# A fourth pair of output tiles by seven quarter products, and a new order of the products in two pairs

## The chip, the core and the metric

The kernel runs on one core of one Trainium2 chip. The metric is the device time of one execution in microseconds: 726.66 us in the median of three runs before the change (726.62 to 727.09). The engines are PE (TensorE, matrix products, with its weight loads shown apart as PEld), DVE (VectorE), ACT (ScalarE), POOL (GpSimd) and SP (SyncE, which here only issues DMAs). They run side by side and wait for each other through semaphores. Each engine takes its own instructions strictly in order.

## The reference: what is computed

One layer of a decoder trunk, for one sequence of 1024 tokens and 1024 channels, in float32:

```
h  = rmsnorm(x) * (1 + scale(c)) + shift(c)
cv, cg, cs, lx, ls = split(h @ w_in)              # 5 x 1024 columns
v  = layernorm(causal_depthwise_conv31(cv * sigmoid(cg)))
y_conv = (silu(v) @ pw2 + b) * silu(cs)
xs = causal_depthwise_conv4(lx)
r, i = sigmoid(blockdiag(xs, wr)), sigmoid(blockdiag(xs, wi))
hs = linear_scan(a(r), sqrt(1 - a^2) * i * xs)
y_lru = hs * silu(ls)
x = x + (1 + gate(c)) * (concat(y_conv, y_lru) @ w_out)
out = rmsnorm(x)
```

The change concerns the product of `y_lru` (1024 channels, the "lru" half) with its half of `w_out`: 1024 x 1024 by 1024 x 1024.

## The kernel before, in words

**Layout.** Activations lie with channels on the 128 partitions and the 1024 tokens along the free axis: eight tiles of 128 x 1024. A matmul multiplies a 128 x 128 block of weights with 128 x 512 of an activation and adds into PSUM. Float32 accuracy is had by splitting each operand into a high part (rounded to fp32r) and a low part (the remainder): a product is three matmuls, high by high ("H"), high weight by low operand ("X") and low weight by high operand ("W"). Names follow this: `whi` and `wlo` for weights, `yh` and `yl` for the eight lru activations ("heads").

**Order of work.** All operations are first recorded with a priority and their reads and writes. A planner (`Plan.order`) then replays them with an estimated cost for each, and on every engine takes the ready operation of lowest priority number; this gives each engine one fixed order. A slot is one output tile of a plain product, 48 matmuls; slot n has priority n. Buffers are planned too. There are 47 large buffers of 128 x 1024 (`NBIG`) for activations, pools of two for raw, high and low weights (`raw`, `whi`, `wlo`), and in PSUM three full tiles (`mm`) and two half tiles (`acc`). Some operations must leave a reserve of large buffers free (`SPARE`).

**Stages on PE.** Slots 0 to 39 are the input projection with the small gate products between them. From slot 40 (`B0`) comes the lru half of `w_out`, eight tiles of 128 output channels: two slots for each pair of tiles. From priority 48 (`C0`) comes the pointwise product `pw2`, and from 56 (`D0`) the convolution half of `w_out`. Both of these use seven half-size products for each pair of tiles (tiles `xpw`, `ypw`, `zpw` and `xout`, `yout`, `zout`). Meanwhile DVE, ACT and POOL compute the depthwise convolution (tiles `c`), then its layer norm (tiles `mean`, `lnbc`, `lnss`), then the operands of `pw2` (`quarters`, tiles named `va`, `vb`, `vc`, `vT` with `h` or `l` for high or low). TLATE is by how much the operands that need differences stand behind the others in priority there and in the same function for the last stage.

**Pairs of lru tiles.** `lru_pair` (L1383 on) treats two output tiles together (`LRU_P = 3` pairs, then the last two tiles as plain slots 46 and 47). Of the eight contraction tiles, heads 0 to 3 (`JS = (0, 1)`, two couples) go by a Strassen-Winograd scheme: with the two output tiles, the two contraction tiles of a couple and the two halves of the tokens, each a 2 x 2 block matrix, seven quarter products stand for eight. Heads 4 to 7 go plainly. `LORDER` names the steps of a pair. Step p multiplies heads 4 to 7 for the first tile (24 matmuls, PSUM tile `lp`). q and r do so for the second tile's two token halves (12 each). 1, z, 2, 3, y, s and 4 are the quarter products of six matmuls each:

```
1: A11 B11 -> lx      z: A12 B21 -> lp       s: S4 B22 -> lp
2: S2 T2  -> lx       y: S1 T1  -> ly       3: S3 T3  -> lx     4: A22 T4 -> lx
```

A and S are weights (S are sums and differences of blocks), B whole operands and T differences of operands. After most steps the accumulator is copied out (`use`): the first copy into a block of the result `acc` is made by ACT with a scale, later ones are added by DVE. Later steps go on accumulating into the same PSUM tile, so they wait until it has been read: q follows y in `ly`, 3 follows 2 and 4 follows 3 in `lx`.

**Operands.** `lru_sums` makes the differences T for each couple (tiles `yhs`, `yls`). The S weights are prepared once, early, in `lru_prepare` (tiles `lz`, `lh`, `ll`, from slot `PREN = 5`), stored to DRAM (`lsdh`, `lsdl`) and loaded again as `lsh`, `lsl` before their pair. Other weights of a tile come as `raw`; ACT copies them to `whi`, writes the negated high part into `wlo`, and a DMA from POOL's queue adds the raw weights to that (`remainder`). With `LWB = "big"` high and low weights of all lru tiles take large buffers. `SPILL` lists finished convolution tiles that are stored to DRAM (`cd`) and loaded back (`cr`) to free their large buffer in between. `acc_store` adds a finished tile `acc` to a copy of x in DRAM.

Of the kernel before, what the change touches and what calls it, by code (L numbers as in the profile page):

```python
# [14 lines left out]
P = 128  # L15
D = 1024
T = 1024
KT = D // P
H = 512
# [21 lines left out]
SPARE = 5  # L41
# [5 lines left out]
UK = 7  # L47
HRES = 2
POOLED = (1, 3, 5)
TLATE = 2.5  # L50
QGATES = ((1, 5), (3, 0), (3, 2), (3, 4))
OUT_P = (0, 1, 2, 3)
HELD = (1, 2, 3)
# [23 lines left out]
NP = {0: (6, 0, 1), 512: (6, 0, 7), 768: (6, 0)}  # L77
SUMS = (2, 0, 4, 3, 1, 6, 7, 5)
CSD = 2
SPILL = (0,2,4)  # L80
SPP0, SPP1, SPN = 30, 40.5, 39
EVN = 4
CQR = 2
YHEADS, YSLOT = 2, 36
JS = (0, 1)
LRU_P = 3
NJ = len(JS)
LK = tuple(2 * j + z for z in (0, 1) for j in JS) + tuple(k for k in range(KT) if k // 2 not in JS)
LACT = ((0, 0), (0, 1), (1, 0), (1, 1))
LORDER = "p1zy2q3s4r"  # L90
LTP = 0.5
LTD = (2,1)
PREN, PRES = 5, 3
PREP, XCP = 18, 19
# [1 line left out]
XCN = 33  # L96
LEV = ()
LWB = "big"
LWO = 0.5
FINP = -0.5  # L100
BCLATE = False
BEHIND = 0
PLACED = ("big",)
MARGINS = 2.0
TERMS = {**{("pw2_0", c): ("HW", "X") for c in "1z"}, **{(f"out_{p}", "1"): ("HX", "W") for p in (0, 1, 2, 3)}, **{(f"pw2_{p}", "1"): ("HX", "W") for p in (1, 2, 3)}}
LTERMS = {}
LLATE = 45
SLOTT = {46: ("HX", "W"), 47: ("HX", "W")}
FINQ = 0.0
LRV = ()  # L110
# [250 lines left out]
def hymba_layer(ctx: ExitStack, tc: tile.TileContext, xT, vecs, mod_w, w_first, w_in,  # L361
# [25 lines left out]
    S = Plan(pools)  # L387
# [117 lines left out]
    B0, C0, D0 = 40, 48, 56  # L505
# [610 lines left out]
    v, c = {}, {}  # L1116
# [160 lines left out]
    def gates(i, n):  # L1277
        xs, xh, xl = lru[i]
        hi, lo = gw.pop(i)
        r, g, a = big_buf(f"r{i}"), big_buf(f"g{i}"), big_buf(f"a{i}")  # L1280
        for j, (dst, b) in enumerate(((r, "br"), (g, "bi"))):
            ps = mm_tile(f"gate{i}_{j}")

            def emit(j=j, ps=ps):
                for lhs, rhs, st in ((hi, xh, 0), (hi, xl, 1), (lo, xh, 2)):
                    for c0, c1 in FULL:
                        pe.matmul(ps()[:, c0:c1], lhs()[:, j, :], rhs()[:, c0:c1],  # L1287
                                  start=st == 0, stop=st == 2)
# [13 lines left out]
        t = sls.pop(i)  # L1302
        TT(pr, "DVE", t, t, r, ALU.mult, r=[t, r], w=[t])
        yh[i], yl[i] = big_buf(f"yh{i}", F32R, 2), big_buf(f"yl{i}", F32R, 2)
        o = split(B0 - 2 + 0.2 * i, yh[i], yl[i], t, reserve=SPARE)
        if i < YHEADS:
            waiting.append(o)
        if LRU_P and i // 2 in JS:
            ys[i] = t
            if i % 2:  # L1310
                lru_sums(i // 2)

    def lru_sums(j):
        pr, x0, x1 = B0 - 2 + 0.4 * j + LTP, ys[2 * j], ys[2 * j + 1]

        def sub(to, a, b):
            TT(pr, "DVE", half(*to), half(*a), half(*b), ALU.subtract, H, r=[a, b], w=[to])
        sub((x0, 0), (x0, 1), (x0, 0))
        sub((x0, 1), (x1, 1), (x0, 1))
        sub((x1, 1), (x1, 1), (x0, 0))  # L1320
        sub((x1, 0), (x1, 0), (x1, 1))
        sets = []
        for z, x in enumerate((x0, x1)):
            hi, lo = (big_buf(f"y{h}s{j}{z}", F32R, 2) for h in "hl")
            if j in LTD:
# [57 lines left out]
    def lru_pair(p, n, use, firsts):  # L1383
# [1 line left out]
        s0, s1 = ("lru", 2 * p), ("lru", 2 * p + 1)  # L1385
        q = n - 1.4 - LWO
        for s in (s0, s1):
            w_bufs(s, LWB)
            DMA(n - 2.5 - LWO, k3(raw[s]), lambda s=s: wsrc(s)[:, :, :], FULL_BYTES, w=[raw[s]])
        r0, r1 = raw[s0], raw[s1]  # L1390
        for s, k in ((s0, 0), (s1, NJ)):
            hi, lo, r = whi[s], wlo[s], raw[s]
            cut = lambda b, k=k: (lambda: k3(b)()[:, k:, :])
            keys = lambda b, k=k: [(b, i) for i in range(k, KT)]
            ACT(q, cut(hi), cut(r), "copy", (KT - k) * P, r=keys(r), w=keys(hi))
# [16 lines left out]
        def quarter(c, a, b, ps, h, begin):  # L1412
            wh, wl, i, key = wq[a]
            rk = [(wh, key), (wl, key)] if key is not None else kk(wh, i) + kk(wl, i)
            for j, (bh, bl) in enumerate(lsets[b]):
                def emit(j=j, bh=bh, bl=bl):
                    o = (i * NJ + j) * P
                    for lhs, rhs, t in ((wh, bh, 0), (wh, bl, 1), (wl, bh, 2)):
                        pe.matmul(half(ps, h)(), lhs()[:, o:o + P], half(*rhs)(),  # L1419
                                  start=begin and j == 0 and t == 0, stop=j == NJ - 1 and t == 2,  # L1420
                                  skip_group_check=True)
                o = S.op("PE", 3 * (H + 32) / 2400, emit, n + g, [*rk, bh, bl],
                         [(ps, h if ps.parts > 1 else 0)], columns=3 * H)
                ops.setdefault(c, o)

        for c in LORDER:
            g += 0.12
            if c == "p":
                groups = LTERMS.get(p, ("HXW",))
                for gr in groups:  # L1430
                    for k in rest:
                        o = mm_k(n + g, p0, s0, yh, yl, k, FULL, first=rest[0], group=gr,
                                 end=gr == groups[-1])
                        ops.setdefault(c, o)
            elif c == "q":
# [84 lines left out]
    for s in slots[4:]:  # L1520
# [5 lines left out]
        if s[0] == "pair":  # L1526
# [3 lines left out]
            def use(n, i, h, ps, key, s=s, ts=ts, begun=begun):  # L1530
                m, to, tk = 2 * s[1] + i, half(ts[i], h), (ts[i], h)
                if (i, h) not in begun:
# [5 lines left out]
                    return  # L1538
                STT(n + 0.5, to, ps, gate1[:, m:m + 1], to, ALU.mult, ALU.add, H,
                    r=[tk, key, ("gate1", m)], w=[tk])  # L1540
            started[n], started[n + 1] = lru_pair(s[1], n, use, [started[n - 2]])
            for m, t in zip((2 * s[1], 2 * s[1] + 1), ts):
                acc_store(n, m, t)
            n += 1
            continue
        if s not in NEXT:
            if s[0] == "lru":
                weights(s, n=n - LWO, eng="DVE" if s[1] in LRV else "DMA", where=LWB,
                        later=[started[LLATE]] if LLATE else [])
            else:  # L1550
                weights(s, late=[pending_evac[n]] if n in pending_evac else ())
# [243 lines left out]
```

## Time and profile before

| what | value |
|---|---|
| median of three runs | 726.66 us |
| the profiled execution | 726.9 us |
| its span, first to last instruction | 725.1 us |
| granted clock of TensorE, mean | 0.995 |
| PE, matmuls | 717.0 us busy, 99% |
| DVE | 617.8 us, 85% |
| ACT | 480.8 us, 66% |
| POOL | 170.8 us, 24% |
| HBM read, written | 79.37 MB, 21.50 MB |

The profile shows one execution. Busy time is what an engine spent in instructions; DMA-issuing ones are not counted. A row of the chain of waits has a start, a duration, and what the time went to; a row of the timeline adds the line in the kernel, the operation, `output<-inputs`, shapes, and how many instructions were merged. Matmuls overlap, so their pitch (start to start) is shorter than the duration of each. The share of busy time is a mean over stages, so each stage is looked at by itself.

### The profile page before, as it was taken

How to read it: one execution, taken by the hardware profiler on the slowest of the kernel's cores; microseconds unless marked ns; L12 is line 12 of the kernel's file. 1: busy time of each engine (PE TensorE's matmuls, PEld its weight loads, DVE VectorE, ACT ScalarE, POOL GpSimd, SP SyncE). 2: the span in 40 equal slices, each digit the busy share in tenths (PEclk: the TensorE clock that was granted, in tenths of full speed). 3: DMA queues.
4: the chain of work that ended last, by engine and by line, in shares of the span. 5: the costliest groups of instructions: out<-in, count | busy, mean ns of one | idle time of the engine just before them, and what ended most of it. 6: DMA issues, size and time to landing. Idle time of an engine off the chain costs nothing.

```text
span 725.1 us, 9076 instructions
## 1 busy us (share of the span) xinstructions
PE 717.0 (99%) x3274; PEld 597.5 (82%) x3274; DVE 617.8 (85%) x848; ACT 480.8 (66%) x615; POOL 170.8 (24%) x172
## 2 busy tenths in 40 slices
PE   9999999999999999999999999999999999999996
PEld 8888888888888888888888888888888888888885
DVE  7999999899799997688499995999789566999656
ACT  7650679655698857966949879858785345755322
POOL 0036233443543320233220220211021101100003
PEclk9999999999999999999999999999999999999997
DMA  9946348768899997799999597998867855774006
GB/s 341 408 169 169 43 112 234 191 120 200 180 246 209 264 220 194 172 221 217 193 217 301 111 188 172 253 239 230 190 103 160 228 120 143 223 190 176 23 17 215
DMA packets 46059, 137.80 MB, mean 190 GB/s; under 512 B 5200, under 2 KB 15824, under 8 KB 45904
## 3 DMA queue, kind: packets, MB, share of 16 engines
q0 software_dynamic: 20016, 54.84, 42.0%
q1 hardware_dynamic: 24992, 81.48, 32.3%
q10 hardware_dynamic: 1008, 0.92, 0.4%
q8 instruction: 25, 0.41, 0.2%
q14 instruction: 18, 0.15, 0.1%
HBM read 79.37 MB, written 21.50 MB: 139 GB/s over the span
## 4 chain that ended last, share of the span: by engine, by line
PE 96%; DVE 1%; ACT 1%; DMA 1%; issue 0%; POOL 0%; POOLq 0%
PE ps L560 57%; PE xout L736 6%; PE xpw L736 6%; PE first L867 5%; PE ypw L736 3%; PE gate L1287 3%; PE lp L560 2%; PE lx L1419 2%; PE zout L736 2%; PE zpw L736 2%; PE ly L560 1%; PE lx L560 1%; PE lp L1419 1%; PE yout L736 1%; PE late L867 1%; PE ly L1419 1%
## 5 line engine op out<-in xcount | busy, mean ns | idle before, releaser
L560 PE MATMUL ps<-uh,whi 128*128 128x512 f32 x576 | 177.4, 389 | 0.0
L560 PE MATMUL ps<-ul,whi 128*128 128x512 f32 x576 | 177.4, 389 | 0.0
L560 PE MATMUL ps<-uh,wlo 128*128 128x512 f32 x576 | 177.3, 389 | 0.0
L560 PEld LDWEIGHTS ps<-uh,wlo 128*128 128x128 f32 x576 | 108.1, 188 | 22.5
L560 PEld LDWEIGHTS ps<-ul,whi 128*128 128x128 f32 x576 | 108.1, 188 | 22.4
L560 PEld LDWEIGHTS ps<-uh,whi 128*128 128x128 f32 x576 | 108.0, 188 | 22.3
L405 ACT CAST whi<-raw 128x1024 fp32r<-128x1024 f32 (+1 forms) x44 | 45.1, 1031 | 48.7 <-PE ps L560 30.0
L437 POOL DMA_DIRECT2D es<-cq x45 | 41.0, 910 | 128.7 <-ACT cq L413 90.2
L432 POOL TENSOR_TENSOR wlo<-raw,whi 128x1024 fp32r<-128x1024 f32 x16 | 41.6, 2607 | 88.6 <-ACT whi L405 88.3
L413 ACT ACT_TABLE_LOAD x45 | 57.7, 1283 | 2.0 <-PEq L1787 0.7
L424 DVE SCALAR_TENSOR_TENSOR cacc<-v,V,cacc 128x511 f32<-128x511 f32 (+14 forms) x75 | 55.8, 744 | 0.5
L424 DVE SCALAR_TENSOR_TENSOR caccs<-v,V,caccs 128x511 f32<-128x511 f32 (+6 forms) x70 | 52.1, 745 | 2.2 <-ACT caccs L413 1.1
L424 DVE SCALAR_TENSOR_TENSOR caccs<-c,wsum,caccs 128x511 f32<-128x511 f32 (+6 forms) x70 | 52.1, 745 | 0.8
L437 POOL DMA_DIRECT2D oo<-co x39 | 37.0, 980 | 41.3 <-issue 10.6
L413 ACT ACTIVATE cq<-v,V 128x511 f32<-128x511 f32 (+14 forms) x45 | 31.8, 709 | 0.0
L424 DVE SCALAR_TENSOR_TENSOR xs<-ps,V,xs 128x1023 f32<-128x1023 f32 (+2 forms) x24 | 30.7, 1278 | 0.0
L424 DVE SCALAR_TENSOR_TENSOR modw<-modw,sc 128x1024 f32<-128x1024 f32 x23 | 29.6, 1289 | 0.2 <-DMA modw<-in_mod_w_dram 0.2
L413 ACT ACTIVATE cq<-c,wsum 128x512 f32<-128x512 f32 x42 | 29.7, 713 | 0.0
L432 DVE TENSOR_TENSOR wlo<-raw,whi 128x1024 fp32r<-128x1024 f32 x20 | 24.4, 1220 | 5.4 <-ACT whi L405 5.2
L413 ACT ACTIVATE co<-v,V 128x510 f32<-128x510 f32 (+12 forms) x39 | 27.0, 707 | 0.0
L413 ACT ACTIVATE finsq<-fin 128x512 f32<-128x512 f32 (+2 forms) x14 | 7.9, 570 | 27.4 <-DVE fin L424 14.3
L432 POOL TENSOR_TENSOR o<-fin,bc 128x256 f32<-128x256 f32 (+1 forms) x8 | 7.8, 994 | 68.6 <-ACT bc L405 63.0
(413 smaller groups left out, 1585.5 us busy)
## 6 DMA issues: line engine op xcount, KB each, us to landing
raw<-in_w_in_dram SPq DMA_DIRECT2D x36, 512.0 KB, 5.5
modw<-in_mod_w_dram SPq DMA_DIRECT2D x24, 512.0 KB, 9.2
scsd<-scs SPq DMA_DIRECT2D x8, 512.0 KB, 3.7
raw<-in_w_out_dram SPq DMA_DIRECT2D x8, 512.0 KB, 7.7
accd<-acc POOLq DMA_DIRECT2D x8, 512.0 KB, 6.9
rawpw<-in_pw_dram SPq DMA_DIRECT2D x8, 512.0 KB, 4.3
scsr<-scsd SPq DMA_DIRECT2D x8, 512.0 KB, 4.5
rawout<-in_w_out_dram SPq DMA_DIRECT2D x8, 512.0 KB, 3.5
```

The lines of the kernel that those rows point to most:

```text
L405: act.copy(out(), in_())
L413: act.activation(out=out(), in_=in_(), func=func, **kw)
L424: dve.scalar_tensor_tensor(out=out(), in0=in0(), scalar=scalar, in1=in1(), op0=op0, op1=op1, accum_out=accum)
L432: lambda: e.tensor_tensor(out=out(), in0=a(), in1=b(), op=op), prio, r, w,
L437: return S.op("POOL", ISSUE, lambda: pool.dma_start(out(), a(), accum_op=ALU.add), prio, r, w, lag=RATE * n / T, after=after, flight=flight)
L560: pe.matmul(ps()[:, a - off:b - off], k3(lhs)()[:, at, :], rhs[k]()[:, a:b], start=(k == first and lhs is wh and rhs is xh and (a - off) % ...
L736: pe.matmul(half(ps, 0)(), half(*lhs)()[:, j * P:j * P + P], half(*rhs)(), start=start and at == 0 and i == 0, stop=at == len(order) - 1 a ...
L867: pe.matmul(ps()[:, a - off:b - off], fw_part(lhs, k, i * P, i * P + P)(), rhs()[:, a:b], start=k == 0 and lhs is wh and rhs is xh, stop=k ...
L1287: pe.matmul(ps()[:, c0:c1], lhs()[:, j, :], rhs()[:, c0:c1], start=st == 0, stop=st == 2)
L1419: pe.matmul(half(ps, h)(), lhs()[:, o:o + P], half(*rhs)(), start=begin and j == 0 and t == 0, stop=j == NJ - 1 and t == 2, skip_group_che ...
```

## The change

The last two lru tiles become a fourth pair (`LRU_P = 4`), so slots 46 and 47 are a pair too, and the weights' preparation runs for four pairs. In pairs one and two s is done ahead of y (`LORDERS`). In pair one, y, 2, 3 and 4 do the terms with the high operand first for both couples and those with the low operand behind them (`QT`, in `quarter`). In pairs two to four p does the terms of the low weights last (`LTERMS`). High and low weights of tiles 0 to 4 now go to the two-deep pools, those of 5 to 7 to large buffers (`LWBS`). The S weights of pairs two to four are held until the second half of the preceding pair has begun (`LSN`: its product 2, in place of its p). Convolution tile 4 is no longer stored and reloaded (`SPILL`). Some priorities move: TLATE from 2.5 to 3.0, the lru differences from 0.5 to 0 (`LTP`), the lru weights from 0.5 to 0.7 slots ahead (`LWO`). The names `LTJ`, `YORD`, `YSTEP`, `LTDMA` and `LWG` put constants or a switch in place of values that stood in the code.

```diff
-TLATE = 2.5
+TLATE = 3.0
-SPILL = (0,2,4)
+SPILL = (0, 2)
-LRU_P = 3
+LRU_P = 4
 LORDER = "p1zy2q3s4r"
-LTP = 0.5
+LORDERS = {0: "p1zsy2q34r", 1: "p1zsy2q34r"}
+LTP = 0.0
+LTJ = (0.0, 0.4)
+YORD = (0, 1, 2, 3, 4, 5, 6, 7)
+LTDMA = ((1, 0), (1, 1))
+YSTEP = 0.2
-LWO = 0.5
+LWO = 0.7
+QT = {(0, c): ("HW", "X") for c in "y234"}
+LSN = 1
+LWBS = (5, 6, 7)
+LWG = 0
-LTERMS = {}
+LTERMS = {p: ("HX", "W") for p in (1, 2, 3)}
...
         for s in (s0, s1):
-            w_bufs(s, LWB)
+            w_bufs(s, LWB if s[1] in LWBS else None)
...
         def quarter(c, a, b, ps, h, begin):
             wh, wl, i, key = wq[a]
             rk = [(wh, key), (wl, key)] if key is not None else kk(wh, i) + kk(wl, i)
-            for j, (bh, bl) in enumerate(lsets[b]):
-                def emit(j=j, bh=bh, bl=bl):
+            groups = QT.get((p, c), ("HXW",))
+            order = [(g_, j) for g_ in groups for j in range(NJ)]
+            for at, (g_, j) in enumerate(order):
+                bh, bl = lsets[b][j]
+                terms = [{"H": (wh, bh), "X": (wh, bl), "W": (wl, bh)}[t] for t in g_]
+
+                def emit(j=j, at=at, terms=terms):
                     o = (i * NJ + j) * P
-                    for lhs, rhs, t in ((wh, bh, 0), (wh, bl, 1), (wl, bh, 2)):
+                    for t, (lhs, rhs) in enumerate(terms):
                         pe.matmul(half(ps, h)(), lhs()[:, o:o + P], half(*rhs)(),
...
-        for c in LORDER:
+        for c in LORDERS.get(p, LORDER):
...
-            started[n], started[n + 1] = lru_pair(s[1], n, use, [started[n - 2]])
+            started[n], started[n + 1] = lru_pair(s[1], n, use, [started[n - LSN if s[1] else n - 2]])
...
-                weights(s, n=n - LWO, eng="DVE" if s[1] in LRV else "DMA", where=LWB,
+                weights(s, n=n - LWO, eng="DVE" if s[1] in LRV else "DMA",
+                        where=LWB if s[1] in LWBS else None,
```

More of the change, by code (lines that the diff above doesn't have):

```diff
@@ L1304, in gates @@
         yh[i], yl[i] = big_buf(f"yh{i}", F32R, 2), big_buf(f"yl{i}", F32R, 2)
-        o = split(B0 - 2 + 0.2 * i, yh[i], yl[i], t, reserve=SPARE)
+        o = split(B0 - 2 + YSTEP * YORD.index(i), yh[i], yl[i], t, reserve=SPARE)
         if i < YHEADS:
@@ L1313, in lru_sums @@
     def lru_sums(j):
-        pr, x0, x1 = B0 - 2 + 0.4 * j + LTP, ys[2 * j], ys[2 * j + 1]
+        pr, x0, x1 = B0 - 2 + LTJ[j] + LTP, ys[2 * j], ys[2 * j + 1]
         def sub(to, a, b):
@@ L1324, in lru_sums @@
             hi, lo = (big_buf(f"y{h}s{j}{z}", F32R, 2) for h in "hl")
-            if j in LTD:
+            if (j, z) in LTDMA:
                 ACT(pr, hi, x, "copy", r=[x], w=[hi], reserve=SPARE + 1)
@@ L1394, in lru_pair @@
             keys = lambda b, k=k: [(b, i) for i in range(k, KT)]
-            ACT(q, cut(hi), cut(r), "copy", (KT - k) * P, r=keys(r), w=keys(hi))
+            ACT(q, cut(hi), cut(r), "copy", (KT - k) * P, r=keys(r), w=keys(hi),
+                after=[started[n - LWG]] if LWG and p else [])
             if s[1] in LRV:
@@ L1414, in quarter @@
             rk = [(wh, key), (wl, key)] if key is not None else kk(wh, i) + kk(wl, i)
-            for j, (bh, bl) in enumerate(lsets[b]):
-                def emit(j=j, bh=bh, bl=bl):
+            groups = QT.get((p, c), ("HXW",))
[4 more added lines that the diff above has]
+                def emit(j=j, at=at, terms=terms):
                     o = (i * NJ + j) * P
-                    for lhs, rhs, t in ((wh, bh, 0), (wh, bl, 1), (wl, bh, 2)):
+                    for t, (lhs, rhs) in enumerate(terms):
                         pe.matmul(half(ps, h)(), lhs()[:, o:o + P], half(*rhs)(),
-                                  start=begin and j == 0 and t == 0, stop=j == NJ - 1 and t == 2,
+                                  start=begin and at == 0 and t == 0,
+                                  stop=at == len(order) - 1 and t == len(terms) - 1,
                                   skip_group_check=True)
-                o = S.op("PE", 3 * (H + 32) / 2400, emit, n + g, [*rk, bh, bl],
-                         [(ps, h if ps.parts > 1 else 0)], columns=3 * H)
+                rd = [x for x in rk if x[0] is wh and g_ != "W" or x[0] is wl and "W" in g_]
+                rd += [bh] * (g_ != "X") + [bl] * ("X" in g_)
+                o = S.op("PE", len(g_) * (H + 32) / 2400, emit, n + g, rd,
+                         [(ps, h if ps.parts > 1 else 0)], columns=len(g_) * H)
                 ops.setdefault(c, o)
-        for c in LORDER:
+        for c in LORDERS.get(p, LORDER):
             g += 0.12
```

## The prediction

> **What bounds the kernel now.** The page comes first: busy shares, chain by engine, then busy time by stretch.
>
> ```profile
> span 725.1 us, 9076 instructions
> PE 717.0 (99%) x3274; PEld 597.5 (82%) x3274; DVE 617.8 (85%) x848; ACT 480.8 (66%) x615; POOL 170.8 (24%) x172
> PE 96%; DVE 1%; ACT 1%; DMA 1%; issue 0%; POOL 0%; POOLq 0%
> 58.00:125.00 67.00, 67.00 (x305) 55.71 (x304) 66.14 (x126) 43.68 (x59) 22.92 (x21) 1.00 0.52 128
> 440.00:470.00 30.00, 30.00 (x134) 24.85 (x133) 22.00 (x24) 27.43 (x32) 5.22 (x6) 1.00 0.83 218
> 470.00:492.00 22.00, 21.90 (x97) 17.82 (x96) 20.72 (x25) 13.62 (x17) 3.49 (x4) 1.00 0.93 252
> 536.00:558.00 22.00, 22.00 (x98) 18.22 (x98) 21.76 (x28) 15.71 (x21) 3.55 (x4) 1.00 0.62 107
> 704.00:725.00 21.00, 14.21 (x109) 13.36 (x107) 14.52 (x32) 5.67 (x14) 7.76 (x8) 0.83 0.57 200
> ```
>
> A stretch row gives its length, busy PE, weight loads, DVE, ACT, POOL, the granted clock, DMA share and GB/s. TensorE is the bound: 96% of the chain, at full clock, busy for every microsecond up to the closing normalisation but for a tenth of one in 470 to 492. So a matmul left out is time gained, and a wait on PE is time lost, one for one. DVE is the second limit (66.14 of 67 us, 21.76 of 22), hence the engine to watch.
>
> Next the chain of waits in order of time, the list of who waited (weight loads), and the timeline of PE at the one place in the lru stage where it stopped.
>
> ```profile
> 538.93 19.04 PE ps L560 x84
> 703.85 0.76 DVE o L424
> PEld ly L560 <- ACT acc L413: 0.5, 1, 0.5
> PEld xout L736 <- DVE fin L424: 0.4, 1, 0.4
> 477.18 0.39 PE L1419 MATMUL lx<-yhs,lsl 128*128 128x512 f32 x1
> 477.66 0.50 PE L560 MATMUL ly<-yh,whi 128*128 128x512 f32 x1
> 478.00 0.39 PE L560 MATMUL ly<-yl,whi 128*128 128x512 f32 x1
> ```
>
> The first row gives the price of a matmul of 512 columns in this stage: 19.04 / 84 = 0.2267 us from start to start. PE gives up the chain only at 703.85, where DVE's scaling takes over; what lies behind runs after the last large product and shifts with it. The three timeline rows are pair one: after the start at 477.18 the next matmul could start at 477.41 and starts at 477.66 (0.25 lost), and its follower comes 0.34 behind it instead of 0.23 (0.11 lost): 0.36 us. It is product y's block, which ACT must copy out before the plain product q adds to the same accumulator.
>
> **The change part by part.**
>
> *The fourth pair.* Two lru tiles as plain slots are 2 x 8 contraction tiles x 3 terms x 2 halves = 96 matmuls. As a pair they are 24 (p), 12 (q), 12 (r) and 7 quarter products x 2 x 3 = 42: 90. Six matmuls go: 6 x 0.2267 = 1.36 us, all on the path. The bounds are 0 (waits eat it) and 1.36.
>
> [...]
>
> *Its evacuations.* They change engine and number.
>
> ```profile
> L413 ACT ACTIVATE acc<-lx,gate x6: 667/676/690, 473.4 to 539.5; 128x512 f32<-128x512 f32 x6
> L413 ACT ACTIVATE acc<-ly,gate x6: 668/681/690, 476.9 to 532.4; 128x512 f32<-128x512 f32 x6
> L424 DVE SCALAR_TENSOR_TENSOR acc<-lx,gate,acc x6: 744/746/751, 479.7 to 533.4; 128x512 f32<-128x512 f32 x6
> L446 DVE TENSOR_SCALAR acc<-ps,gate x2: 1282/1283/1284, 549.0 to 559.5; 128x1024 f32<-128x1024 f32 x2
> 558.40 1.22 DVE L432 TENSOR_TENSOR vlb<-c,vhb 128x1024 fp32r<-128x1024 f32 x1
> 562.34 1.07 PE L736 MATMUL zpw<-vlb,whipw 128*128 128x512 f32 x4
> ```
>
> Three pairs made 12 ACT copies, so a pair makes four and four DVE additions. The fourth pair puts 4 x 0.68 = 2.7 us on ACT (15.71 of 22 us busy there) and 4 x 0.746 - 2 x 1.283 = 0.42 us on DVE, which is full there. That DVE work stands between the layer norm and the pw2 products. The last low part of B21 is done at 558.40 + 1.22 = 559.62 and is first wanted by the fourth of the matmuls at 562.34, at 563.02: 3.4 us of cover. PE will arrive 1.7 us sooner and DVE 0.4 later, so 1.3 remain and I cost this at 0. If the cover is gone, each microsecond that DVE is late is lost on PE. The later difference operands (TLATE 3.0) move further behind the whole ones on DVE, which favours the two products that come first; cost 0, with ends of 0 and the 1.3 us by which DVE's cover could then be short at the third.
>
> *Preparing the fourth pair's weights*, after slot 5, by DMA and ACT.
>
> ```profile
> L437 POOL DMA_DIRECT2D lz<-in_w_out_dram x12: 853/878/1237, 63.0 to 106.0; - x12
> L413 ACT ACTIVATE lz<-lz x9: 400/405/418, 62.3 to 97.7; 128x256 f32<-128x256 f32 x9
> L405 ACT CAST lh<-lz x3: 1038/1041/1047, 109.0 to 117.0; 128x1024 fp32r<-128x1024 f32 x3
> L413 ACT ACTIVATE ll<-lh x3: 1048/1050/1065, 115.1 to 120.5; 128x1024 fp32r<-128x1024 f32 x3
> L437 POOL DMA_DIRECT2D ll<-lz x3: 859/859/879, 116.6 to 122.0; - x3
> lsh<-lsdh SPq DMA_DIRECT2D x3, 512.0 KB, 5.1
> lsl<-lsdl SPq DMA_DIRECT2D x3, 512.0 KB, 5.9
> cr<-cd SPq DMA_DIRECT2D x3, 512.0 KB, 5.7
> ```
>
> A third of these rows: on ACT 3 x 0.405 + 1.04 + 1.05 = 3.3 us, on POOL five more issues (4 x 0.88 + 0.86 = 4.4 us), on SP one load and two stores. In 58 to 125 ACT has 23 us free, POOL 44, and PE waits for neither. The issues stand ahead of the convolution's own accumulating DMAs on POOL's queue, whose results are wanted some 350 us later. Cost 0; without that cover at most ACT's 3.3 us; a gain there is excluded, since nothing leaves.
>
> *The S blocks.* SP gains two loads for pair four (5.1 and 5.9 us to land) and loses the store and the reload of conv tile 4 (the cr row). The loads of pairs two to four now wait for the preceding pair's product 2, 48 matmuls into pair one, 470 + 48 x 0.2267 = 480.9. Behind SP's three, now two, reloads they land by about 495; pair two begins after 90 matmuls, at 490.3, and its s wants them 36 matmuls later, near 498.5. Cost 0, cover some 3 us. Conv tile 4 instead holds one of the 47 large buffers, while the low and high weights of lru tiles 0 to 4 leave that pool (four in the first pair): on balance buffers come free, and the operand splits, which must leave five or six in reserve, can go sooner.
>
> *Order in pairs one and two.* Product s, of whole operands, comes ahead of y, and in pair one y, 2, 3 and 4 take the terms of the high operand first. The whole of 2 (6 matmuls, 1.36 us) can then lie between y and q, where ACT needs 0.68 to copy. I take the 0.36 us as gained; the ends are 0.36 gained and, if 4 waits directly behind 3 for DVE's addition (0.75) in both pairs, 1.5 lost. Pair two's p, whose accumulator is free as soon as s is read, can fill that hole, so I go by the gain.
>
> *Moved priorities.* The difference operands of heads 0 to 3 go half a slot earlier on DVE and ACT (LTP), ahead of the parts of heads 4 to 7, which p multiplies.
>
> ```profile
> 478.59 1.23 DVE L432 TENSOR_TENSOR yl<-sls,yh 128x1024 fp32r<-128x1024 f32 x1
> ```
>
> The last of these parts ends at 479.8 already now, 9.9 us after p began, and PE fills the time with 1, z, y and 2; now it has s as well. Cost 0, ends 0 and one such operation, 1.2 lost. In pairs two to four p's terms of the low weights go last (LTERMS): 16 matmuls, 3.6 us, more time for those weights, a help without a price. LWO brings the weights' priorities forward by a fifth of a slot; YORD, YSTEP, LTJ, LTDMA and LWG restate what the code did: 0 for all.
>
> *Weights in the two-deep buffers.* This is the new wait. The second tile's high and low weights in pair one take over those of slot 39.
>
> ```profile
> 459.50 0.61 PE L560 MATMUL ps<-ul,whi 128*128 128x512 f32 x2
> 469.47 0.62 PE L560 MATMUL ps<-uh,wlo 128*128 128x512 f32 x2
> 480.49 0.82 ACT L405 CAST whi<-raw 128x768 fp32r<-128x768 f32 x1
> 481.35 0.85 ACT L413 ACTIVATE wlo<-whi 128x768 fp32r<-128x768 f32 x1
> 482.60 0.88 POOL L437 DMA_DIRECT2D wlo<-in_w_out_dram x1 [0.74 <-ACT wlo L413]
> wlo<-in_w_out_dram POOLq DMA_DIRECT2D x3, 384.0 KB, 8.4
> DMA to landing us min/median/max: 5.3/7.1/9.0
> ```
>
> Slot 39 ends at 469.9. Cast, negation and issue take, by the 480.49 chain, 2.1 us to the issue; landing 8.4: ready at 480.4 at the earliest. Product q wants it after 54 matmuls, at 482.1: a cover of 1.7 us (4.8 with the 5.3 us landing, 1.1 with 9.0), less what ACT has queued (27.43 of 30 us busy just before). The same holds at pair two's q. Behind the negation on POOL's queue stand the other accumulating DMAs; on PE the whole rest of the pair. I take 0 (the median landing leaves cover); the ends are 0 and, with three ACT operations of 1.05 ahead in each pair, 2 x (3.2 - 1.7) = 3.0 lost.
>
> **Sum.** -1.36 - 0.36 = -1.72 us. Against its own execution (726.9 us, 1.8 around the span) that is 725.2; the median of the runs shown is 0.24 below that execution, so the forecast is 726.66 - 1.72 = 724.9.
>
> **The rivals.** *Gain absorbed.* If DVE reaches the pw2 operands late, or pair one's wait comes back elsewhere, the six matmuls turn into waiting. DVE's 99% in 536 to 558 speaks for it, 3.4 us of cover against. If the cover is 1.3 short, the time is 724.9 + 1.3 = 726.2, within noise of before.
>
> *Late weights, slower.* Place: q of pairs one and two; price: lateness over the 1.7 us of cover, paid twice. It decides once both together exceed 1.72 (no gain) and 3.2 (slower by 0.2%); with ACT three to four operations behind, 724.9 + 2 x (4.2 - 1.7) = 729.9, and at three operations 727.9. For it speaks ACT's load at 440 to 470; against it that PE follows its static order almost without gaps in the same stretch now. [...]
>
> *The stall stays.* Only the matmuls pay: 725.3.
>
> **How the numbers follow.** What a measurement here can tell from no change is about 0.2%, 1.45 us: below 725.2 faster, above 728.1 slower. Forecast 0.42 (724.3 to 725.2; lower by the 0.4 us wait at xout at most plus 0.2 scatter); the stall stays 0.13 and absorbed 0.18, both within; late weights 0.27, nearly all slower, down to 727.9. That gives faster 0.42, same 0.32, slower 0.26. The range of 8 in 10 is 724.3 to 728.8; the likeliest case's own is 724.3 to 725.6.
>
> **What would show it.** 3268 matmuls instead of 3274; chain rows for lp, lx, ly where ps stood before xpw; xpw's first matmul near 556.2 instead of 557.97; no wait of ly on ACT acc; closing normalisation near 702.1. Wrong: a weight-load wait on wlo (a DMA) at ly L560, or on DVE vlb at zpw; a stretch between 470 and 558 in which PE is under full; or a later first xpw.

## The result

The changed kernel takes 729.75 us (median of six runs, 728.96 to 730.24) against 726.9 us for the kernel before in the same session (six runs, 726.62 to 727.23): a ratio of 1.0039, 95% interval 1.0026 to 1.0052. It is 2.85 us slower. Forecast were 724.9 us and a range up to 728.8.

### The profile page after: what moved, and what is told of

It reads as the page before. It is cut to its first block, busy times and chain, and to the rows that moved or that the text cites. A ratio compares the mean times of both kernels' runs of the same rounds, so it can differ in the third digit from the quotient of the medians.

```text
span 727.9 us, 9083 instructions
## 1 busy us (share of the span) xinstructions
PE 717.2 (99%) x3268; PEld 596.7 (82%) x3268; DVE 619.6 (85%) x850; ACT 484.4 (67%) x623; POOL 175.4 (24%) x177
## 4 chain that ended last, share of the span: by engine, by line
PE 88%; issue 4%; DVE 4%; DMA 3%; ACT 1%; POOL 0%; DVEq 0%; POOLq 0%; ACTq 0%
PE ps L569 50%; PE xout L745 6%; PE xpw L745 6%; PE first L876 5%; PE ypw L745 3%; PE gate L1296 3%; PE y L715 2%; PE lx L1434 2%; PE zpw L745 1%; PE zout L745 1%; DMA yls<-sls 1%; DMA wlo<-in_w_out_dram 1%; PE lx L569 1%; PE yout L745 1%; PE lp L569 1%
## 5 line engine op out<-in xcount | busy, mean ns | idle before, releaser
L433 DVE SCALAR_TENSOR_TENSOR modw<-modw,sc 128x1024 f32<-128x1024 f32 x23 | 32.5, 1416 | 0.0
```

The costliest lines, as they stand in the source:

```text
L433: dve.scalar_tensor_tensor(out=out(), in0=in0(), scalar=scalar, in1=in1(), op0=op0, op1=op1, accum_out=accum)
```

## The profile after

The first fence has rows of the page (span, busy time, chain by engine) and then the busy time by stretch, in the columns of the prediction. The stretch 504 to 518 is new.

```profile
span 727.9 us, 9083 instructions
PE 717.2 (99%) x3268; PEld 596.7 (82%) x3268; DVE 619.6 (85%) x850; ACT 484.4 (67%) x623; POOL 175.4 (24%) x177
PE 88%; issue 4%; DVE 4%; DMA 3%; ACT 1%; POOL 0%; DVEq 0%; POOLq 0%; ACTq 0%
58.00:125.00 67.00, 67.00 (x304) 55.75 (x303) 66.15 (x125) 44.04 (x62) 27.53 (x26) 1.00 0.57 140
470.00:492.00 22.00, 20.77 (x92) 16.73 (x91) 19.66 (x25) 12.13 (x15) 3.50 (x4) 1.00 1.00 271
504.00:518.00 14.00, 12.62 (x55) 10.07 (x55) 9.71 (x10) 9.74 (x12) 3.54 (x4) 1.00 1.04 264
```

The six matmuls are gone: 3268 instead of 3274. The early stretch carries the fourth pair's preparation at no cost to PE (67.00 of 67 us). But PE, which had 21.90 of 22 us in 470 to 492, now stands for 1.23 us there and for 1.38 us in 504 to 518, where the kernel before lost nothing. DMA has 3% of the chain instead of 1%, and the DMA share of 470 to 492 rose from 0.93 to 1.00. (PE's share of the chain fell from 96% to 88% because the chain is followed back from the two late transfers to the issues, ACT and DVE behind them; PE itself was idle for far less.) What stopped PE is in the list of who waited (place, releaser, us in all, times, longest) and in PE's timeline; the bracket is idle time and releaser.

```profile
PE lp L569 <- DMA wlo<-in_w_out_dram: 1.4, 1, 1.4
PE lx L1434 <- DMA yls<-sls: 1.2, 1, 1.2
484.32 0.39 PE L569 MATMUL ly<-yh,wlo 128*128 128x512 f32 x1
485.94 0.50 PE L1434 MATMUL lx<-yls,lsh 128*128 128x512 f32 x1 [1.23 <-DMA yls<-sls]
513.35 0.61 PE L569 MATMUL lp<-yl,whi 128*128 128x512 f32 x2
515.34 0.74 PE L569 MATMUL lp<-yh,wlo 128*128 128x512 f32 x2 [1.38 <-DMA wlo<-in_w_out_dram]
556.80 0.50 PE L1434 MATMUL lx<-yhs,whi 128*128 128x512 f32 x1 [0.21 <-DVE acc L433]
561.01 0.39 PE L745 MATMUL xpw<-vha,whipw 128*128 128x512 f32 x1
```

From start to start, less the pitch of 0.2267: 485.94 - 484.32 - 0.23 = 1.39 us before the last high-weight terms of product 2 of pair one, which multiply the difference operand `yls` of the second couple; 515.34 - 513.58 - 0.23 = 1.54 us before the low-weight terms of p of pair three (tile 4); 0.37 us before product 4 of pair four, behind DVE's addition of 3. Each wait costs its follower another 0.11 (the next start 0.34 behind it instead of 0.23). Together 3.63 us. The first matmul of `xpw` starts at 561.01; 556.2 was forecast.

How much of the whole this is shows in one length, which a later or earlier beginning does not touch: the time from the first matmul of the lru pairs to the first of the last stage (`xout`). The first two rows are of the kernel before, the others of the changed one.

```profile
469.92 0.62 PE L560 MATMUL lp<-yh,whi 128*128 128x512 f32 x2
631.25 0.39 PE L736 MATMUL xout<-yha,whiout 128*128 128x512 f32 x1
```

```profile
470.95 0.39 PE L1434 MATMUL lx<-yh,whi 128*128 128x512 f32 x1
634.63 0.39 PE L745 MATMUL xout<-yha,whiout 128*128 128x512 f32 x1
```

161.33 us became 163.68: 2.35 more ("the stage" below). Taking every start-to-start distance there above the usual pitch as lost, PE lost 0.61 us before and 4.33 after: 4.33 - 0.61 - 1.36 (six matmuls) = 2.36. In these two executions the stage also begins 1.03 later, and what lies behind it is 0.53 shorter; the 1.03 belongs to the clock at the start of an execution and not to the change (last section). What makes up the other 0.5 of the 2.85 between the medians is not settled.

Why the two transfers came late is in the order of ACT, on POOL's queue, in the transfers' times to land (shortest, median, longest of the two `yls`), and on SP's queue. Kernel before, then changed kernel:

```profile
468.68 1.05 ACT L413 ACTIVATE yls<-yhs 128x1024 fp32r<-128x1024 f32 x1
470.13 0.87 POOL L437 DMA_DIRECT2D yls<-sls  x1 [2.11 <-ACT yls L413]
DMA to landing us min/median/max: 5.6/5.8/6.1
478.70 0.39 PE L1419 MATMUL lx<-yls,lsh 128*128 128x512 f32 x1
505.04 0.87 POOL L437 DMA_DIRECT2D wlo<-in_w_out_dram  x1 [10.58 <-ACT wlo L413]
517.24 0.61 PE L560 MATMUL lp<-yh,wlo 128*128 128x512 f32 x2
```

```profile
472.39 0.84 ACT L422 ACTIVATE wlo<-whi 128x768 fp32r<-128x768 f32 x1
473.88 0.87 POOL L446 DMA_DIRECT2D wlo<-in_w_out_dram  x1 [6.91 <-DVE yl L441]
474.99 1.05 ACT L422 ACTIVATE yls<-yhs 128x1024 fp32r<-128x1024 f32 x1
476.44 0.86 POOL L446 DMA_DIRECT2D yls<-sls  x1 [1.69 <-ACT yls L422]
DMA to landing us min/median/max: 8.4/8.9/9.5
475.53 0.43 SPq L460 DMA_DIRECT2D lsh<-lsdh  x1
476.15 1.55 SPq L460 DMA_DIRECT2D lsl<-lsdl  x1
477.81 1.07 SPq L460 DMA_DIRECT2D cr<-cd  x1
480.16 0.33 SPq L460 DMA_DIRECT2D raw<-in_w_out_dram  x1
505.95 1.79 POOL L446 DMA_DIRECT2D wlo<-in_w_out_dram  x2 [5.97 <-ACT wlo L422]
```

Before, the second `yls` left at 470.13, landed 5.6 us later at 475.7 and was wanted at 478.70: 3.0 us of cover. Now it leaves at 476.44, 6.31 us later. POOL's queue did not hold it, for POOL was idle for 1.69 us ahead of it (the bracket); it waited for ACT's negation, which starts at 474.99 instead of 468.68. In ACT's order the cast and negation of tile 1's weights (the negation at 472.39) now stand among the operands; that the two-deep buffers and the moved priorities put them there is likely, but was not tested by itself. PE's order wants the transfer at 484.55, 5.85 us later than before. And it flies 9.5 us, 3.9 longer: 3.0 - 6.31 + 5.85 - 3.9 = -1.4, the wait.

In its flight SP loads two S blocks, a convolution tile and raw weights. The S blocks were meant to be held until product 2 of pair one, but `LSN` holds them only in the planner's replay, and no semaphore holds SP: they leave at 475.5.

The low weights of tile 4 have another sum. Before, they left at 505.04, flew 7.54 us and were wanted at 517.24, 4.66 us after the landing. Now they leave at 505.95 (0.91 later), fly 9.35 us (1.81 longer) and are wanted at 513.81, 3.43 earlier, since p of pair three has moved forward with its low-weight terms at its end: 4.66 - 0.91 - 1.81 - 3.43 = -1.49. The replay had counted 6.0 us of flight (`LAND`) and 1.0 for the issue (`ISSUE`). With these 7.0 us both would have landed in time, at 483.4 and 512.95, and so they would have with the flights of the kernel before, at 482.0 and 513.5.

So the theory: PE's fixed order asks for two accumulating transfers before they land, since they fly about 9.4 us instead of the 7 of the plan. Rivals: the fourth pair's own work (additions, preparation) costs the time; the new order of the products does; or it came from one execution.

## Experiments

**The changed kernel once more** (no edit).

> The changed kernel once more, for one further profiled execution. If its two waits are set by the order and by the company of the transfers, both stand again at the same places: product 2 of pair one on the sum's transfer (1.0 to 2.0 us) and p of pair three on the low weights of tile 4 (1.0 to 2.0 us), with flights of 8.5 to 10 us; if they came from that one execution, at most one of them is over 0.5 us.

```profile
PE lx L1434 <- DMA yls<-sls: 1.4, 1, 1.4
PE lp L569 <- DMA wlo<-in_w_out_dram: 1.2, 1, 1.2
```

Both waits stand again, with flights of 9.6 and 9.2 us, and the stage has 163.69 us. It was one run, of 730.4 us. The waits belong to the order, not to an execution.

**Later places in the order.** Only the planner's estimate of a flight changes, so that PE's order asks for these operands later; the computation stays as it is.

```diff
+LW, LY = 6, 9
-    def remainder(prio, lo, hi, src, n, rk, wk, sk=(), reserve=0, after=()):
+    def remainder(prio, lo, hi, src, n, rk, wk, sk=(), reserve=0, after=(), flight=LAND):
...
-        ADD(prio, lo, src, n, r=[*wk, *sk], w=wk, flight=LAND)
+        ADD(prio, lo, src, n, r=[*wk, *sk], w=wk, flight=flight)
...
-                remainder(pr, lo, hi, x, T, [hi], [lo], [x], SPARE)
+                remainder(pr, lo, hi, x, T, [hi], [lo], [x], SPARE, flight=LY)
...
-                remainder(q, cut(lo), cut(hi), lambda s=s, k=k: wsrc(s)[:, k:, :], (KT - k) * P, keys(hi), keys(lo))
+                remainder(q, cut(lo), cut(hi), lambda s=s, k=k: wsrc(s)[:, k:, :], (KT - k) * P, keys(hi), keys(lo), flight=LW)
```

First with 9 for `yls` alone (the diff above):

> The changed kernel with another constant in the planner: the flight of the two DMAs that make the low parts of the lru differences is put at 9 us instead of 6; the work is the same. Theory (PE's fixed order asks for two landings too early): product 2's low terms stand some 3 us later in PE's order, the wait of 1.4 us in pair one goes, and the one at pair three's p may move, since the order behind it changes: 1.3 to 3 us faster than the changed kernel. Rival (the fourth pair's own copies and additions load ACT and DVE, and that is where the time goes): the wait turns up elsewhere, within 0.7 us of the changed kernel.

It took 727.12 us (ratio to before 1.0004, 0.9995 to 1.0013; 727.17 us before in that session). The second `yls` flew 9.7 us, and nothing waited for it; nor did p of pair three wait. One wait is new: product q of pair two, which adds to y's tile, waits for the low weights of tile 3, which flew 9.2 us. This is one of the two places that the prediction's rival *late weights* had named:

```profile
PE ly L570 <- DMA wlo<-in_w_out_dram: 1.2, 1, 1.2
```

Then with 7 for the low weights of the pairs too (`LW, LY = 7, 9`):

> As the run before, and the flight of the DMAs that make the low weights of the lru tiles at 7 us instead of 6. Theory: both long waits go; what is left is the 1.36 us of matmuls and pair one's old wait of 0.36, less 0.5 at pair four's product 4: 725.4 to 726.0, that is 0.9 to 1.5 us under the kernel before. Rival (copies and additions): no better than 728.5.

726.3 us, ratio 0.9988 (0.9979 to 0.9996): 3.45 below the changed kernel (3.7 when each is taken against the kernel before in its own session) and a little faster than the kernel before; 0.3 above the time expected. Its stretches 470 to 492 and 504 to 518 and the ends of the stage:

```profile
470.00:492.00 22.00, 22.00 (x97) 17.79 (x97) 20.14 (x25) 12.15 (x15) 3.50 (x4) 1.00 0.97 261
504.00:518.00 14.00, 13.95 (x78) 11.80 (x77) 9.17 (x12) 8.37 (x12) 3.50 (x4) 1.00 1.05 273
470.95 0.39 PE L1435 MATMUL ly<-yhs,lsh 128*128 128x512 f32 x1
487.80 0.39 PE L1435 MATMUL lx<-yls,lsh 128*128 128x512 f32 x1
631.23 0.39 PE L746 MATMUL xout<-yha,whiout 128*128 128x512 f32 x1
```

160.28 us of stage, 0.92 lost. The second `yls` leaves at 476.44 as in the changed kernel, and the transfers are as slow (`yls` 9.7, tile 4's weights 9.5), but PE wants `yls` at 487.80 instead of 484.55, and the time is back. So it was the place in the order: the fourth pair, its additions and its preparation are all in this kernel. Pair four's wait on DVE (0.48 with its follower) is gone too, as the whole order was planned anew.

More of the same does not bring more. With 7.5 and 10 and the S blocks planned earlier again (behind p of the preceding pair instead of its product 2):

```diff
-LSN = 1
+LSN = 2
+LW, LY = 7.5, 10
```

> The changed kernel with the planner's flights at 7.5 us (low weights of lru tiles) and 10 us (low parts of the lru differences), and the S loads placed a slot earlier again (LSN = 2). Theory (PE's fixed order asks for landings too early): with more time still at the places where run e3_flight9w7 kept waits of 0.5 and 0.4 us, at the level of that run or under it, 725.6 to 726.5. Rival (longer assumed flights only push the waits on): 726.8 or more, with a new wait of over 0.5 us on PE.

727.03 us (ratio 1.0011, 0.9998 to 1.0025; single runs 726.01 to 730.97). A miss, above the time expected: waits of 0.3 to 0.5 us stand at a layer-norm step (`lnbc`) and at q of pair two in place of those removed, and the runs scatter. The four runs of twelve above 729 us have a mean granted clock of 0.991 to 0.993, the other eight one of 0.996 to 0.998; the last section comes back to this.

With three more moves of the order on top of e3's estimates:

```diff
-LORDERS = {0: "p1zsy2q34r", 1: "p1zsy2q34r"}
+LORDERS = {0: "p1zsy2q34r", 1: "p1zs2y3q4r", 3: "p1zy2s3q4r"}
-LTERMS = {p: ("HX", "W") for p in (1, 2, 3)}
+LTERMS = {p: ("HX", "W") for p in (0, 1, 2, 3)}
```

> The kernel with the longer flights of e3 (low weights of the lru 7 us, sums of the inputs 9 us), with three more moves that keep operands with differences away from the place where they become ready: pair two computes product 2 behind y, pair four in the order p, 1, z, y, 2, s, 3, 4, and p of pair one puts its low-weight terms at its end, as the others do. By the theory of the landings (the change lost its time where the order of the TensorE asks for a transfer before it has landed) the waits of e3 at y on the low weights of pair two (0.33 us) and at y on the VectorE's addition (0.24) should go, and the time be 725.4 to 726.4, 0 to 0.9 below e3's 726.3. By the rival, that the change's extra additions and evacuations cost time whatever the order, it stays at 726.3 or above.

726.57 us (ratio 0.9995, 0.9986 to 1.0004). The wait of pair two on the low weights (at q, in y's tile) is gone as expected, but the stage (160.42 us) is not shorter than e3's: pieces of 0.1 us took its place. The time missed its expectation by 0.2 and lies where the rival had put it; the rival's ground, that additions and evacuations cost time whatever the order, is answered by e3, which has them all.

**Company of the transfer.** Here SP is truly held: it stores one element of pair one's result to a place that nobody reads, which must wait for that result, and only then loads pair two's S blocks; what stands behind them on SP's queue waits too (the convolution tile's load leaves at 483.12 instead of 477.81).

```diff
+    pair_acc, mark = {}, dram.tile([1, 1], F32, tag="mark", name="mark")
...
-            DMA(n - 2.2, lambda t=t: t().bitcast(F32), lambda h=h: s_d[h, p], FULL_BYTES, r=[("ls", h, p)], w=[t], after=firsts)
+            def load(h=h, t=t):
+                if h == "h" and p == 1:
+                    sp.dma_start(mark, pair_acc[0][0]()[0:1, 0:1])
+                sp.dma_start(t().bitcast(F32), s_d[h, p])
+            S.op("SP", max(0.1, FULL_BYTES / 360e3), load, n - 2.2, [("ls", h, p)], [t], after=firsts)
...
+            pair_acc[s[1]] = ts
```

In the changed kernel:

> The changed kernel with one thing added: ahead of pair two's load of the high S weights SP stores one element of pair one's result, so that this load and everything behind it on SP's queue really wait until product z of pair one has been added in (near 482 us), where the written order has them; at present SP, which nothing stops, starts them at 475.5. Theory (late landing by company): the second low part of the lru differences, issued at 476.4, then flies 6 to 7 us instead of 9.5, PE's wait of 1.4 us at product 2 of pair one goes, 1.2 to 1.5 us faster than the changed kernel. Rival (late issue): it flies 9 us whatever flies beside it, the wait stays over 1 us, time within 0.4 us of the changed kernel. Both: the wait at pair three's p stays.

729.12 us (ratio 1.003, 1.0018 to 1.0041), 0.6 below the changed kernel, less than the 1.2 to 1.5 expected. The S blocks leave at 482.2 and 482.7, the second `yls` flies 7.8 us instead of 9.5, and its wait is gone. But at p of pair three PE stands longer in the profiled execution: 2.30 from start to start instead of 1.54. PE arrives there 1.29 us earlier and the weights leave 1.30 us earlier, so the longer wait is their longer flight, 10.1 us instead of 9.3.

```profile
482.20 0.35 SPq L1419 DMA_DIRECT2D lsh<-lsdh  x1
DMA to landing us min/median/max: 7.8/7.8/7.9
PE lp L569 <- DMA wlo<-in_w_out_dram: 2.1, 1, 2.1
```

So the second `yls` flew 9.5 us with the S blocks beside it and 7.8 without. This execution took 731.32 us, the longest of six (the others 728.44 to 729.5), with a stretch at half clock behind the wait (granted clock 0.50 in each of the slices from 516 to 519; last section), so its stage is not that of the median. What lengthens the flight of tile 4's weights was not tested. The same hold in e3's kernel, whose order wants nothing at that time:

> e3 with the wait of e1: SyncE stores one element of pair one's sum before it loads the S blocks of pair two. By the theory of company (a transfer flies longer because SyncE's loads run beside it) the second transfer of the sums flies 7 to 8 us instead of some 9, but in e3's order nothing waits for it, so the time moves by less than 0.5 us from e3's 726.3: 725.8 to 726.8. If the loads of the S blocks come late for the carries of pair two, or meet the low weights of the next tiles, as they did in e1, a wait of 0.5 to 2 us appears at y or p of pairs two and three, and the time is 727 to 728.5. By the rival (the flight does not matter for the time) nothing but the flight changes.

726.26 us (ratio 0.9989, 0.998 to 0.9998). The flight fell from 9.7 to 7.2 us, and the time is e3's. What keeps it above the 5.6 us of the kernel before, with the S blocks held, stays open.

```profile
DMA to landing us min/median/max: 7.2/7.4/7.5
470.71 0.39 PE L1440 MATMUL ly<-yhs,lsh 128*128 128x512 f32 x1
630.65 0.39 PE L746 MATMUL xout<-yha,whiout 128*128 128x512 f32 x1
```

Its stage takes 159.94 us, and PE loses 0.59 us there, as the kernel before did (0.61). With equal losses the difference to 161.33 is what the six matmuls are worth: 1.39 against 1.36 reckoned (the losses are counted with the same pitch, so this is an account that closes and not a second measurement).

The reverse in the kernel before: three stores of 512 KB ahead of the second `yls`, to a place that nobody reads.

```diff
+    beside = [dram.tile([P, T], F32, tag=f"beside{k}", name=f"beside{k}") for k in range(3)]
...
+                if z == 1:
+                    o = S.ops[-1]
+
+                    def accompanied(emit=o.emit, hi=hi):
+                        for k in range(3):
+                            sp.dma_start(beside[k], hi().bitcast(F32))
+                        emit()
+                    o.emit = accompanied
```

> The kernel before with three more stores of 512 KB each on SP's queue, of the high part of the second lru difference tile to DRAM that nobody reads, started just ahead of that tile's accumulating DMA (flight 5.6 us before). It measures by itself what company costs such a DMA. Theory: the flight grows to 8 to 10 us, and PE's product 2 in pair one, which had 3 us to spare, waits 0 to 1.5 us. Rival (flights do not depend on company): it stays under 6.5 us and the time within 0.3 us of the kernel before.

731.62 us (ratio 1.0069, 1.0056 to 1.0082). Issued at 470.58, the transfer lands 11.4 us later instead of 5.6. Its company is more than the stores: a load of raw weights, which left at 461.59 before, is pushed behind them to 469.73. PE stands at the very place where the changed kernel stood; more than expected.

```profile
468.16 1.52 SPq L1335 DMA_DIRECT2D beside<-yhs  x3
DMA to landing us min/median/max: 6.1/8.7/11.4
482.03 0.50 PE L1429 MATMUL lx<-yls,lsh 128*128 128x512 f32 x1 [2.71 <-DMA yls<-sls]
```

Side by side, `yls` flew 9.5 and 9.7 us with the S blocks beside it (changed kernel, e3) and 7.8 and 7.2 without (e1, e10), and 11.4 with three stores and the pushed load beside it and 5.6 without (e8, before). In what way the company lengthens a flight was not shown.

**Parts undone.** Three pairs instead of four in the changed kernel (`-LRU_P = 4`, `+LRU_P = 3`):

> The changed kernel with three pairs again (LRU_P = 3), the other edits kept: the last two tiles are plain slots. Theory (late landings, which come from the moved issues and the two-deep weights, not from the fourth pair's arithmetic): the waits of 1 us and more in pairs one to three stay, the six matmuls come back: 729.5 to 731. Rival (the fourth pair's own work costs the time): back to 726.5 to 727.5.

730.0 us (ratio 1.0036, 1.0024 to 1.0049): no faster without the fourth pair. Two waits on low weights stand there too, at other places:

```profile
PE lx L1434 <- DMA wlo<-in_w_out_dram: 1.0, 1, 1.0
PE ly L569 <- DMA wlo<-in_w_out_dram: 0.9, 1, 0.9
```

The same edit in e3's kernel:

> Run e3_flight9w7 with three pairs (LRU_P = 3): what the fourth pair alone is worth where landings are in time. Theory: six matmuls of 0.2267 us more, 1.36 us over that run, 727.5 to 728.2. Rival (the fourth pair's evacuations take the gain away): within 0.5 us of that run.

729.62 us (ratio 1.0033, 1.0021 to 1.0045), a miss: the order shifted with the edit, and p of pair three waits for its weights again (1.0 us). It does not price the fourth pair alone. e10 against the kernel before comes nearer, but has all the other edits of the change too.

Last, e3's kernel with the old order of the products:

```diff
-LORDERS = {0: "p1zsy2q34r", 1: "p1zsy2q34r"}
+LORDERS = {}
-QT = {(0, c): ("HW", "X") for c in "y234"}
+QT = {}
```

> Run e3_flight9w7 without LORDERS and QT: all pairs in the old order, s behind 3, every term with its operand. What the new order alone is worth where landings are in time. Theory: pair one's product 2 needs the low part of the differences again before y's and q's turn, and 4 waits for the copy behind 3; 0.4 to 1.5 us over that run, 726.7 to 727.8. Rival (the order is worth nothing, flights were all): within 0.3 us of that run.

729.47 us (ratio 1.0034, 1.0021 to 1.0047), 3.2 above e3, more than expected:

```profile
PE lx L1435 <- DVE acc L434: 2.6, 3, 1.2
```

Products that add to `lx` stand right behind DVE's reading of it, at 505.9, 552.8 and 556.5. The last two are in pair four, whose steps this edit leaves as they are: with their followers 1.9 us were lost there because the planner moved things. So the new order is no cause of the loss, for e3 has it and does not lose; what it saves by itself this run does not price.

The stage, the flights and the losses in this table are of one profiled execution each, whose own time stands beside the median.

| kernel | time, median, us | profiled execution, us | stage, us | second `yls`: flight, PE loses | tile 4's low weights: flight, PE loses |
|---|---|---|---|---|---|
| before | 726.9 | 726.9 | 161.33 | 5.6, none | 7.5, none |
| changed | 729.75 | 730.24 | 163.68 | 9.5, 1.39 | 9.3, 1.54 |
| e1, S blocks held | 729.12 | 731.32 | 164.81 | 7.8, none | 10.1, 2.30 |
| e2, 9 for `yls` | 727.12 | 728.08 | 161.75 | 9.7, none | 9.4, none |
| e3, and 7 for weights | 726.3 | 726.76 | 160.28 | 9.7, none | 9.5, none |
| e9, and order moved | 726.57 | 726.17 | 160.42 | 10.4, none | 9.6, none |
| e10, e3 and held | 726.26 | 726.21 | 159.94 | 7.2, none | 9.9, none |
| e8, before with stores | 731.62 | 731.64 | 165.95 | 11.4, 2.89 | not looked at |

## Why the prediction was wrong

*The six matmuls*, -1.36: right (3268, and 1.39 in e10). *Pair one's stall*, -0.36: right as forecast for the changed kernel, where no matmul of `ly` waits for ACT's copy; in e3 and e10 0.24 of it returns, for DVE's addition.

*Preparation and evacuations*, 0: right. POOL took 27.53 us instead of 22.92 in 58 to 125 (4.6 more, 4.4 reckoned) and PE lost nothing there; at the `pw2` operands, where the absorbed-gain rival had its wait, PE lost 0.15 us (at `xpw`, for ACT). That rival's price was misread: the 1.3 us were the cover that remained, and the prediction then used them as what the cover falls short by. The price of one product directly behind another's addition, which I put in pairs one and two, came in pair four: 0.48 us.

*The S blocks*, 0: wrong in its ground. I read the hold of `LSN` as a wait on the chip; SP ran ahead and issued at 475.53 instead of 480.9. The loads themselves were not late, but they flew beside the second `yls`. The step asked only when they land, not whose flight they lengthen; holding them took 1.7 and 2.5 us off the flight of `yls` (e1, e10).

*Moved priorities*, 0 with an end of 1.2: wrong. I followed the `yl` parts that p multiplies and not the last difference operand, which went out 6.31 us later. The low-weight terms at the end of p (`LTERMS`) were "a help without a price": the planner spent that help by moving p of pair three forward, so that its low weights were wanted 3.4 us earlier than before, and PE stood there. *Weights in the two-deep buffers*, "I take 0 (the median landing leaves cover)": this is the step that failed. It took the flights of before (8.4 and the bounds 5.3 to 9.0) into an order with other company, and looked at q alone. The cover at q held: in the changed kernel q of pairs one and two did not wait; tile 1's weights landed in 6.2 us. What waited for landings was product 2 on `yls` and p of pair three on tile 4's weights: 1.50 and 1.65 us with their followers. With the flights of before, 5.6 and 7.5 us instead of 9.5 and 9.3, neither would have.

By the sum PE would lose 0.61 - 0.36 = 0.25 us in the stage. It lost 4.33: the three waits with their followers, 3.63, and 0.70 in pieces of about 0.1. So 4.08 us were missing from the sum: -1.72 + 4.08 = 2.36, the stage's change. The rival *late weights* had the kind (a landing behind the place in PE's order) and nearly the size (3.0 at its end), at two other places, and it put the lateness on ACT's queue where the runs show the flight and the order. So the nearness of its 727.9 to 729.9 us to the measured 729.75 is chance. Its place q of pair two did wait in other orders: 1.32 us in e2, 1.10 in e4.

## What to carry to other kernels

Where a planner fixes an engine's order from assumed flights, a change that moves a transfer must be priced with the flight it will have among its new neighbours (9.5 us here, where the kernel before had 5.6), and each operand's last transfer followed to the instruction that wants it, not only the weights that the change names. A hold that exists only in the plan does not hold a queue on the chip (SP issued the S blocks at 475.53, not at the 480.9 of the prediction). One to three microseconds more of allowance for the flight, without any change of the computation, were worth 3.45 us here, and turned a change that lost into one that gains a little.

## What the runs showed of the hardware

After some waits TensorE ran at half clock (0.50) for about 3.4 us, which costs more than the wait seems to: in e8 every matmul from 483.5 to 486.9 took 0.43 us instead of 0.23, 1.6 us in all. Stretches of that kernel, then of the changed one:

```profile
480.09:483.51 3.42, 1.48 (x6) 1.24 (x7) 0.87 (x3) 2.51 (x3) 0.87 (x1) 1.00 1.02 380
483.51:486.92 3.41, 3.41 (x9) 2.65 (x8) 2.97 (x5) 0.10 (x1) 0.88 (x1) 0.50 1.04 297
512.33:515.74 3.41, 2.03 (x10) 1.37 (x9) 3.38 (x4) 1.81 (x3) 0.13 (x1) 1.00 1.05 265
515.74:519.15 3.41, 3.41 (x19) 2.84 (x18) 0.71 (x1) 0.00 (x0) 1.41 (x2) 1.00 1.06 266
```

A slow stretch came after 2.89 us lost in e8, 2.30 in e1 and 1.19 in e6, but not after 1.39 and 1.54 in the changed kernel; e5 had one with no single loss above 0.5. So these stretches do not sort by the length of the wait. In the clock's own record the full clock lasted, until it fell, a whole number of steps of 3.413 us (before: 713.39 us, 209 steps; changed kernel: 716.80 us, 210; e8: from 5.64 to 483.51, 140), and each of the four slow stretches was about 3.4 us, one step, long. Cut into such steps, the step ahead of each of the four has few columns in it, counted by the matmuls that start there (512 each for most): 1040 (e6), 2560 (e1), 3072 (e8) and 3088 (e5, beside many small layer-norm matmuls). In the kernel before and the changed one, which have no slow stretch there, the steps from 60 to 700 us hold 3979 or more; at the usual pitch a step holds some 7700 (an estimate: 3413 / 226.7 x 512). The changed kernel's waits left 4096 (the wait of 1.54) and, as the end of a step at 485.02 divided the wait of 1.39, 6144 and 5632. In these executions the slow stretches thus go with little work in a step. The steps do not begin at the same time in each (4.32 us in the kernel before, 5.64 in e8, 7.15 in the changed kernel), so by the author's estimate from e8 the same wait may cost 1.6 us more in one execution than in the next, as the clocks of e5's runs suggest (0.991 to 0.993 in the four above 729 us).

The executions also begin differently. The sixteen matmuls of `c_row` took 2.65 us in the profiled execution of the kernel before and 3.75 in that of the changed one, and all later work stood 1.03 us later; over all profiled executions they took 2.65 to 3.76. Here too it is the clock. From start to start these matmuls of 128 columns, and those of `token_stats` behind them, stand 213 ns apart at first and 111 ns from 4.3 us on in the one and from 7.15 us on in the other, where the record of the clock begins with the full clock (4.32 and 7.15). The first row is of the kernel before:

```profile
3.01 2.65 PE L828 MATMUL c_row<-ident,cs 128*128 128x128 f32 x16
3.08 3.75 PE L837 MATMUL c_row<-ident,cs 128*128 128x128 f32 x16
```

The other executions go the same way: where `c_row` took 2.65 to 2.70 us the lru stage begins at 469.9 to 470.1 (before, e2, e6, e9), with 3.23 and 3.24 at 470.37 and 470.34 (e8, e7), with 3.49 and 3.67 at 470.58 and 470.71 (e4, e10), and with 3.75 and 3.76 at 470.9 to 471.1 (the changed kernel twice, e1, e3), whichever kernel it is. So a microsecond between two profiles is not yet the change, and lengths within a stage compare better than times of day.
